# Scores of two heads per step, a shorter way out of the router, and the last norm's vector by DMA, in a one-core transformer kernel

## The chip, the cores and the metric

The kernel runs on one core of one Trainium2 chip. The metric is the device time of one execution in microseconds. Engines are named as in the profile: PE (TensorE matmuls), PEld (its weight loads), DVE (VectorE), ACT (ScalarE), POOL (GpSimd) and SP (SyncE, which issues nearly all the DMAs). In the rows below a matmul of 32-bit operands leaves two records, so a count of x32 stands for 16 matmuls.

## The reference, cut to what matters

256 tokens of width 1024 pass a first block (a forget-gate attention of 16 heads, two squared-ReLU feed-forwards, a latent attention) and a second one (a gated unit with a differential attention of 4 heads, an attention into 256 memory tokens, and 32 experts). All is float32.

```python
# first block, the mixer that the change touches (16 heads of 64)
proj = h @ w_in;  cum = jnp.cumsum(jax.nn.log_sigmoid(f_logit), axis=1)
s = jnp.einsum('bqhd,bkhd->bhqk', q_blk, k) * scale
s = s + jnp.transpose(c_blk, (0, 2, 1))[..., None] - c_keys[:, :, None, :]   # then causal softmax, @ v
...
# second block, differential attention: two softmax maps per head, 64 wide
s = jnp.einsum('bhiqd,bhikd->bhiqk', qb, k)
a = p[:, :, 0] - lam * p[:, :, 1]
...
# experts: top-1 of 4 groups, top-2 of the 8 experts in it
pg = jax.nn.softmax(t @ w_rg + b_rg);  gate_g, gidx = lax.top_k(pg, 1)
el = (t @ w_re + b_re).reshape(N, N_GROUPS, EXPERTS_PER_GROUP)[jnp.arange(N), gidx[:, 0]]
pe_top, eloc = lax.top_k(jax.nn.softmax(el), TOP_K)
wts = gate_g * pe_top / jnp.sum(pe_top)
out = sum_k wts[k] * ((silu(x @ w_gate[e]) * (x @ w_up[e])) @ w_down[e])
...
return rms_norm_2(x + out, norm_final)      # the last norm, with its gain vector of 1024
```

## The kernel before, in words

**Dense part (0 to about 834 us).** Activations lie feature-major, 8 chunks of 128 features by 256 tokens. Weights stream in 2 MB chunks through slots of SBUF; SP issues the loads (L395) as slots come free. Each 128x1024 weight block is split into a high half (ACT, `wh`, L420) and a low half (DVE or POOL, `wl`, L426), and PE forms three products per block (L455 to L457).

**Forget-gate attention (`fox`, L777).** Loop over 8 pairs of heads. For a pair PE projects the keys (`fk`, both heads stacked on 128 partitions), a pipeline step runs, PE projects the queries (`fq`), and another step runs. A step takes from each head in flight one stage of four: scores and exponentials (`sa`), normalisation (`sn`), transposes (`sb`), values (`sc`, once per pair). Before, each step holds the scores of one head: `qk_rows` (L623) issues one matmul of 128x128 (L628) and one of 128x256 (L630) on the 64 partitions of that head, into one PSUM bank of the four called `acc`. DVE adds the head's bias `fb` (made ahead on POOL in one of 4 buffers, L797 to L800) and takes the maximum (L595), ACT exponentiates (L597). The differential attention (L1181) issues the scores of its two 64-wide halves in the same way, one half behind the other, in one step.

**Router's end and the first experts (`moe`, L1449).** Behind the logits PE runs ten matmuls that nothing reads (`warm`, L400, line L404), while DVE finds the group and the two experts of each token: `place` (L1467) compares all pairs of n values (is-equal, is-greater), masks the ties, adds the two and sums. The result `asg` goes to PE for the ranks inside the experts (L1500 to L1502); DVE makes the 0/1 matrix `oh` that picks tokens into 32 rows per expert for four experts at once (L1540); PE sums the norms (`slot_rstd`) and gathers the tokens (L1533, 16 matmuls into two banks), DVE scales the gathered rows into `xg` (L1535), then makes the gate weights `wt` and `ow` (L1564 to L1555). `weigh(0)` has PE carry these to the rows (L1513) before the first expert.

**Experts.** Each of 32 experts has three loads of 2 MB (gate, up, down), 96 in all. Eleven slots exist; each is refilled when PE has read it. For an expert: `inner` twice (gate and up, L1620, 16 matmuls), `summed` (L1633), `hidden` (L1636), `permute` (L1609), `down` in two halves (L1653), with results split into `yh` (ACT) and `yl` (DVE); the results are added in four accumulating banks by `combine` (L1667), one expert later. The last expert's loads are cut into 12 parts of 512 KB. After expert 29 `gains` (L1684) spreads the last norm's gain vector over 128 partitions with 8 matmuls against scaled identities; in the last expert there are two warm matmuls before each half of `down`. `finish` (L1698) squares, multiplies by the gain, finds the inverse root, scales and stores two tiles of 512 KB.

The order on each engine is the order in which the code issues it; semaphores are inserted where tiles are shared.

Of the kernel before, what the change touches and what calls it, by code (L numbers as in the profile page):

```python
# [19 lines left out]
D = 1024  # L20
# [16 lines left out]
WARM = dict(router=10, rank=2, hidden=2, down=2)  # L37
# [131 lines left out]
PA.add("gf", 8)  # L169
# [18 lines left out]
def params(i):  # L188
# [23 lines left out]
    put(pa, PA, "gf", feature_major(i["norm_final_2"]))  # L212
# [46 lines left out]
def pack(i):  # L259
# [17 lines left out]
    return dict(wd=wd, we=we, xt=turned(i["x"]), memt=turned(i["mem_2"]), pa=pa, pb=pb, ca=ca, cb=cb, cd=cd)  # L277
# [28 lines left out]
class Program:  # L306
# [279 lines left out]
    def scores(self, qk, bias, st=None):  # L586

        nc = self.nc
        s = self.bank("acc", [128, 384])
        qk(s)  # L590
        l = self.t("L", [128, 384], bufs=2)
# [39 lines left out]

    def run(self):
# [22 lines left out]
        for name in ("sq", "sqt", "ln", "rb", "rmem", "z", "st", "xh", "xl", "memk", "b0"):  # L655
            self.home[name] = self.base
        dense = self.open("dense")
# [119 lines left out]
    def fox(self):  # L777
# [14 lines left out]

        def head(h, q, k, bc, state):
            o = 64 * (h % 2)

# [5 lines left out]

            def sa():
                state[h] = self.scores(lambda s: self.qk_rows(s, [(q[o:o + 64], k[o:o + 64])]), b)
# [304 lines left out]
    def second(self):  # L1108
# [72 lines left out]
        def head(h, q, k):  # L1181
            state = {}

            def sa():
                st = state["s"] = self.t("st2", [128, 12], bufs=3)
                for i in range(2):
                    state[i], _ = self.scores(
                        lambda s: self.qk_rows(s, [(q[64 * i:64 * i + 64], k[64 * i:64 * i + 64])]), ali[:, h],
                        (st[:, 0:4], st[:, 4:8])[i])
# [259 lines left out]
    def moe(self):  # L1449
# [77 lines left out]
        def gather(xg, ohs, rs, n):  # L1527

            for b in range(2):
                p = self.bank("pp", [128, 4, n])  # L1530
                for m in range(4 * b, 4 * b + 4):
                    for t in range(2):
                        mm(p[:, m % 4], xs[:, t, m * 128:m * 128 + 128], ohs[t], start=t == 0, stop=t == 1)  # L1533
                for m in range(4 * b, 4 * b + 4):
                    v.scalar_tensor_tensor(xg[:, m], p[:, m % 4], self.pcol("ffn2", m), rs, op0=OP.mult, op1=OP.mult)  # L1535

        def onehot(e0):
# [9 lines left out]
            gather(xg, [f[:, t] for t in range(2)], rw[:, 0], 128)  # L1547
# [54 lines left out]
        weigh(0)  # L1602

# [42 lines left out]
        def down(w, h, warm=0):  # L1646

            yh, yl = self.t("yh", [128, 1024], F32R), self.t("yl", [128, 1024], F32R)
            for half in range(2):
# [7 lines left out]
                if warm and not half:  # L1657
                    self.warm(warm)
# [23 lines left out]
        r = self.t("fr", [128, 2, 5])  # L1682

        def gains(tag, pool):  # L1684

            g = self.t("gf", [128, 8, 128], tag=tag, pool=pool)
            for half in range(2):
                p = self.bank("ps", [128, 512])
                for j in range(4):
                    d = self.t("gd", [128, 128], tag="sqt", bufs=2)  # L1690
                    v.tensor_scalar(d, self.cst("ident"), self.pcol("gf", 4 * half + j), None, op0=OP.mult)
                    mm(p[:, j * 128:j * 128 + 128], ones, d, start=True, stop=True)
                nc.scalar.copy(g[:, 4 * half:4 * half + 4].rearrange("p a b -> p (a b)"), p)
            return g.rearrange("p a b -> p (a b)")
# [3 lines left out]
        def finish():  # L1698


            def total(t, half):
                c = halves[half]
                sq = self.t("sqo", [128, 512], tag="gs0")
                nc.scalar.activation(sq, comb[t][half], AF.Square, accum_out=r[:, t, half:half + 1])
                v.tensor_mul(o[:, t, c], comb[t][half], gf[:, c])

            def norm(t):
                self.inverse(r[:, t, 3:4], r[:, t, 2:3], D, EPS, r[:, t, 4:5])

            def both(t):  # L1710
                v.tensor_add(r[:, t, 2:3], r[:, t, 0:1], r[:, t, 1:2])

            def scale(t):
                for half, c in enumerate(halves):
                    if t > half:
                        nc.scalar.mul(o[:, t, c], o[:, t, c], r[:, t, 3:4])
                    else:
                        v.tensor_scalar(o[:, t, c], o[:, t, c], r[:, t, 3:4], None, op0=OP.mult)
                nc.sync.dma_start(self.out[t * 128:t * 128 + 128], o[:, t])

            total(0, 0)
            total(0, 1)
            both(0)
            ln = self.inverse_begin(r[:, 0, 3:4], r[:, 0, 2:3], D, EPS, r[:, 0, 4:5])
            total(1, 0)
            total(1, 1)
            ln()
            both(1)
            scale(0)
            norm(1)  # L1730
            scale(1)

# [3 lines left out]
        for e in range(NE):  # L1736
# [107 lines left out]
```

## Time and profile before

| | us |
|---|---|
| median of 3 runs (lowest to highest) | 1298.98 (1298.26 to 1300.97) |
| the profiled execution | 1301.46 |
| its span, first to last instruction | 1299.8 |
| PE busy | 1218.3 (94%) |
| DVE busy | 655.7 (50%) |
| ACT busy | 525.1 (40%) |
| POOL busy | 185.3 (14%) |
| share of the span on the chain that ended last: PE, DVE, DMA | 75%, 9%, 8% |

The page's row of DMA throughput (40 slices of 32.5 us) shows 426 GB/s in most slices from 880 us on, and between 113 and 344 GB/s before. The busy shares are means over stages with different limits: in the dense part PE is nearly always busy, in the experts' part the DMA engines are. How long a wait lasts is read in the stage itself. Weight loads (PEld) overlap the matmuls.

### The profile page before, as it was taken

Reading aid. Unit: us, or ns where it says so; the run is one execution under the profiler, and the core shown is the slowest. Engines: PE = TensorE matmul, PEld = TensorE weight load, DVE = VectorE, ACT = ScalarE, POOL = GpSimd, SP = SyncE. Lnnn points to the kernel's source line nnn. Section 1 sums busy time; section 2 is a strip of 40 time slices with the busy share of each in tenths; the row PEclk is TensorE's granted clock in tenths of the full one; section 3 lists DMA queues with packets and bytes.
Section 4 is the critical chain, followed back from the end, with each engine's and each line's share of the span. In section 5 each row is a group of like instructions: output and inputs, shape, how many; then the busy total and the mean of one; then the engine's idle time right before and its main releaser. Section 6 shows DMA issues by size and latency. Waiting matters only on the chain.

```text
span 1299.8 us, 22284 instructions
## 1 busy us (share of the span) xinstructions
PE 1218.3 (94%) x9292; PEld 986.8 (76%) x9292; DVE 655.7 (50%) x1243; ACT 525.1 (40%) x982; POOL 185.3 (14%) x183
## 2 busy tenths in 40 slices
PE   7999999999989999999989999978999999897986
PEld 7788899999988899999978898944545545544443
DVE  6756666545677575655678875332222222122213
ACT  4645564544554564554555554211121121121213
POOL 4167210000152010000274210100000000000000
PEclk9999999999999999999999999999999999897978
DMA  9453445445433335544455348869999999999994
GB/s 340 192 217 113 165 155 195 157 174 205 178 132 121 126 134 195 195 156 177 187 190 190 136 165 344 333 274 426 426 426 425 424 427 424 426 424 426 427 419 160
DMA packets 30230, 338.10 MB, mean 260 GB/s; under 512 B 3488, under 2 KB 3760, under 8 KB 8112
## 3 DMA queue, kind: packets, MB, share of 16 engines
q1 hardware_dynamic: 30128, 336.66, 65.1%
q8 instruction: 74, 1.21, 0.4%
q14 instruction: 28, 0.23, 0.0%
HBM read 335.58 MB, written 1.06 MB: 259 GB/s over the span
## 4 chain that ended last, share of the span: by engine, by line
PE 75%; DVE 9%; DMA 8%; POOL 3%; ACT 2%; issue 2%; SPq 0%; DVEq 0%; POOLq 0%; ACTq 0%
PE pp L456 9%; PE pp L455 9%; PE pp L457 9%; DMA ring<-in_we_dram 8%; PE pp L1620 7%; PE acc L457 4%; PE acc L456 4%; PE acc L455 4%; PE ps L1633 4%; PE acc L1667 3%; PE pp L1533 3%; PE ps L1653 2%; DVE wl L426 2%; POOL x L900 1%; PE acc L630 1%
## 5 line engine op out<-in xcount | busy, mean ns | idle before, releaser
L426 DVE TENSOR_TENSOR wl<-ring,wh 128x1024 fp32r<-128x1024 f32 (+1 forms) x244 | 304.4, 1252 | 70.7 <-ACT wh L420 70.7
L420 ACT CAST wh<-ring 128x1024 fp32r<-128x1024 f32 (+1 forms) x246 | 252.5, 1029 | 137.5 <-PE acc L456 92.1
L457 PE MATMUL pp<-xh,wl 128*128 128x256 f32 x800 | 226.3, 283 | 1.7 <-DVE wl L426 1.7
L455 PE MATMUL pp<-xh,wh 128*128 128x256 f32 x800 | 227.3, 284 | 0.1
L456 PE MATMUL pp<-xl,wh 128*128 128x256 f32 x800 | 226.5, 283 | 0.3 <-DVE xl L515 0.3
L455 PE MATMUL acc<-hh,wh 128*128 128x256 f32 x560 | 160.0, 286 | 6.7 <-ACT hh L514 6.7
L456 PE MATMUL acc<-hl,wh 128*128 128x256 f32 x560 | 160.9, 287 | 0.7 <-DVE hl L515 0.7
L457 PE MATMUL acc<-hh,wl 128*128 128x256 f32 x560 | 159.8, 285 | 0.6 <-DVE wl L426 0.6
L455 PEld LDWEIGHTS pp<-xh,wh 128*128 128x128 f32 x800 | 151.9, 190 | 2.1 <-issue 1.7
L457 PEld LDWEIGHTS pp<-xh,wl 128*128 128x128 f32 x800 | 150.3, 188 | 1.9 <-DVE wl L426 1.9
L456 PEld LDWEIGHTS pp<-xl,wh 128*128 128x128 f32 x800 | 150.3, 188 | 0.7 <-DVE xl L515 0.6
L1620 PE MATMUL pp<-ring,xg 128*32 128x512 f32 x1024 | 123.4, 620 | 14.1 <-DMA ring<-in_we_dram 11.1
L455 PEld LDWEIGHTS acc<-hh,wh 128*128 128x128 f32 x560 | 108.8, 194 | 6.7 <-ACT hh L514 6.7
L456 PEld LDWEIGHTS acc<-hl,wh 128*128 128x128 f32 x560 | 108.4, 194 | 1.8 <-DVE hl L515 1.7
L457 PEld LDWEIGHTS acc<-hh,wl 128*128 128x128 f32 x560 | 108.8, 194 | 0.8 <-DVE wl L426 0.8
L1624 DVE COPY gs<-pp 128x512 f32<-128x512 f32 x32 | 22.1, 692 | 166.3 <-PE pp L1620 166.3
L1620 PEld LDWEIGHTS pp<-ring,xg 128*32 128x32 f32 x1024 | 30.9, 112 | 88.1 <-issue 81.5
L1633 PEld LDWEIGHTS ps<-ca,gs 128*128 128x128 f32 x512 | 64.8, 205 | 25.8 <-issue 25.4
L1656 DVE TENSOR_TENSOR yl<-ps,yh 128x512 fp32r<-128x512 f32 x64 | 44.3, 692 | 72.8 <-ACT yh L1655 72.8
L456 PE MATMUL pp<-hl,wh 128*128 128x256 f32 x272 | 77.6, 285 | 2.7 <-DVE hl L515 2.2
L455 PE MATMUL pp<-hh,wh 128*128 128x256 f32 x272 | 79.1, 291 | 0.8 <-DVE x L900 0.8
L457 PE MATMUL pp<-hh,wl 128*128 128x256 f32 x272 | 77.2, 284 | 0.7 <-DVE wl L426 0.7
(380 smaller groups left out, 1975.6 us busy)
## 6 DMA issues: line engine op xcount, KB each, us to landing
ring<-in_we_dram SPq DMA_DIRECT2D x76, 2048.0 KB, 29.1
ring<-in_wd_dram SPq DMA_DIRECT2D x58, 2048.0 KB, 8.2
ring<-in_we_dram SPq DMA_DIRECT2D x34, 1024.0 KB, 28.8
ring<-in_we_dram SPq DMA_DIRECT2D x12, 512.0 KB, 14.4
bc<-cdr SPq DMA_DIRECT2D x8, 256.0 KB, 6.3
ring<-in_wd_dram SPq DMA_DIRECT2D x1, 1792.0 KB, 6.8
ring<-in_wd_dram SPq DMA_DIRECT2D x1, 1536.0 KB, 10.8
pb<-in_pb_dram SPq DMA_DIRECT2D x1, 1152.0 KB, 10.7
```

The source lines that it names most:

```text
L420: self.nc.scalar.copy(h[:, :n], w)
L426: eng.tensor_sub(l[:, :n], w, h[:, :n].bitcast(F32))
L455: mm(out, wh, xh, start=start, stop=False, skip_group_check=skip)
L456: mm(out, wh, xl, start=False, stop=False, skip_group_check=skip)
L457: mm(out, wl, xh, start=False, stop=stop, skip_group_check=skip)
L1533: mm(p[:, m % 4], xs[:, t, m * 128:m * 128 + 128], ohs[t], start=t == 0, stop=t == 1)
L1620: mm(p[32 * j:32 * j + 32], xg(k), w(k * 512, k * 512 + 512), start=k < 4, stop=k > 3, tile_position=(0, 32 * j))
L1624: v.tensor_copy(g, p)
L1633: mm(p[:, f], g[:, f * 128:f * 128 + 128], self.cst("fold"), start=True, stop=True)
L1653: mm(p[32 * j:32 * j + 32], h[:, j], w(o, o + 512), start=True, stop=True, tile_position=(0, 32 * j))
L1656: v.tensor_sub(yl[:, c], p, yh[:, c].bitcast(F32))
L1667: mm(acc[t][half], pe[:, t * 128:t * 128 + 128], y[:, half * 512:half * 512 + 512], start=start and not i, stop=stop and i == 1, skip_grou ...
```

## The change

Five edits, all in the order and grouping of work; what is computed stays.

- Scores: a new `qk_pair` issues, for both heads of a pair, the two 128x128 products and then the two 128x256 products, each head on its own 64 partitions and into its own `acc` bank. In `fox` the even head's step does it for both heads and runs both softmaxes; the odd head's step holds no scores. The differential attention uses it for its two halves.
- Router's end: five warm matmuls instead of ten; `place` puts both comparisons in one tile and sums it, without the add; the first gather uses four banks (two of `pp`, two of `ps`) instead of two; `weigh(0)` moves behind the first expert's `inner`.
- Beginning: six warm matmuls before the first projection.
- Last expert: `combine` runs through both token tiles for `yh`, then for `yl`; the warm matmuls before the two halves of `down` are gone, and three stand before each of the two `inner`.
- Last norm: `gains` and its copies are gone; the vector is loaded by one DMA that repeats a row of 4 KB on 128 partitions, issued on SP behind the last weights. `finish` is reordered, and the second tile is stored in two halves, one issued by ACT.

```diff
-WARM = dict(router=10, rank=2, hidden=2, down=2)
+WARM = dict(start=6, router=5, rank=2, last=3)
...
+    def qk_pair(self, q, k):
+        mm = self.nc.tensor.matmul
+        s = [self.bank("acc", [128, 384]) for _ in range(2)]
+        for a, b, n in ((0, 128, 128), (128, 384, 256)):
+            for i in range(2):
+                r = slice(64 * i, 64 * i + 64)
+                mm(s[i][:, a:b], q[r, a:a + 128], k[r, 0:n], start=True, stop=True)
+        return s
...
             def sa():
-                state[h] = self.scores(lambda s: self.qk_rows(s, [(q[o:o + 64], k[o:o + 64])]), b)
+                if h % 2 == 0:
+                    for i, s in enumerate(self.qk_pair(q, k)):
+                        state[h + i] = self.softmax(s, bias[h + i])
...
         def place(name, vals, n):
-            eq, gt = (self.t(name + i, [128, 2, n, n], tag=f"gs{j}") for j, i in enumerate("eg"))
+            both = self.t(name + "e", [128, 2, n, 2 * n], tag="gs0")
+            eq, gt = both[:, :, :, :n], both[:, :, :, n:]
...
-            v.tensor_add(gt, gt, eq)
-            v.tensor_reduce(cnt, gt, axis=AX.X, op=OP.add)
+            v.tensor_reduce(cnt, both, axis=AX.X, op=OP.add)
...
-            gather(xg, [f[:, t] for t in range(2)], rw[:, 0], 128)
+            gather(xg, [f[:, t] for t in range(2)], rw[:, 0], 128, *([("pp", "pp", "ps", "ps")] if e0 == 0 else []))
...
-        weigh(0)
...
             for half in range(2):
-                for t in range(2):
-                    for i, y in enumerate(ys):
+                for i, y in enumerate(ys):
+                    for t in range(2):
                         mm(acc[t][half], pe[:, t * 128:t * 128 + 128], y[:, half * 512:half * 512 + 512], ...
...
+            square(0, 0)
+            square(1, 0)
+            square(0, 1)
+            gain(0, 0)
+            first(0)
+            gain(1, 0)
+            first(1)
+            gain(0, 1)
+            estimate(0)
+            square(1, 1)
+            mean(0)
+            gain(1, 1)
+            newton(0)
+            scale(0, 0, v)
+            scale(0, 1, v)
+            store(0, slice(0, 1024), nc.sync)
+            estimate(1)
+            mean(1)
+            newton(1)
+            scale(1, 1, nc.scalar)
+            scale(1, 0, v)
+            store(1, halves[1], nc.scalar)
+            store(1, halves[0], nc.sync)
...
             for i in range(2):
+                if last:
+                    self.warm(WARM["last"])
                 gs.append(inner(i, w[i], lambda k: xg[:, k, c]))
                 self.load_next(slots[i][1])
...
+            if e == 0:
+                weigh(0)
             h = hidden(gs, rw[:, 1, c])
...
-                self.warm(WARM["hidden"])
...
-                gf = gains(*next(p for _, s in slots for p in s if p[1] is not self.base))
+                gf = self.t("gf", [128, 1024], tag="cd")
+                nc.sync.dma_start(gf, bass.AP(tensor=self.a["gr"].tensor, offset=self.a["gr"].offset,
+                                              ap=[[0, 128], [1, D]]))
```

In `finish`, `square` is ACT's squared sum, `gain` DVE's product with the vector, `first`, `mean` and `newton` are DVE steps on one column, and `estimate` is ACT's logarithm and exponential.

PE in the fox stage, before: the scores of the first two heads (`fk`, `fq`), one head per step, between the projections (`xh`, `xl` with `wh`, `wl`).

```order
L457 MATMUL pp<-xh,wl 128x256
L628 MATMUL acc<-fk,fq 128x128
L630 MATMUL acc<-fk,fq 128x256
L455 MATMUL pp<-xh,wh 128x256
...
L457 MATMUL pp<-xh,wl 128x256
L628 MATMUL acc<-fk,fq 128x128
L630 MATMUL acc<-fk,fq 128x256
L455 MATMUL pp<-xh,wh 128x256
```

The same place now: the scores of a pair in one step (lines are shifted by the edit, L641 is `qk_pair`, L612 the transposes of an earlier head).

```order
L456 MATMUL pp<-xh,wl 128x256
L641 MATMUL acc<-fk,fq 128x128 x2
L641 MATMUL acc<-fk,fq 128x256 x2
L454 MATMUL pp<-xh,wh 128x256
...
L456 MATMUL pp<-xh,wl 128x256
L641 MATMUL acc<-fk,fq 128x128 x2
L641 MATMUL acc<-fk,fq 128x256 x2
L612 MATMUL acc<-ca,P 128x128 x3
```

The second group of the second piece belongs to the next pair: between the two, 16 blocks of projections run where 8 ran before.

PE at the router's end, before: warm matmuls, ranks, norms of the picked rows, gather, weights of the rows (`ow`), first expert.

```order
L404 MATMUL pp<-ones 128x256 x10
L1500 MATMUL ps<-asg,ca 128x32
L1501 MATMUL ps<-asg,ones 128x32
L1502 MATMUL ps<-asg,ca 128x32
L404 MATMUL pp<-ones 128x256 x2
L1513 MATMUL ps<-oh,rc 128x128 x2
L1533 MATMUL pp<-oh,xs 128x128 x16
L1513 MATMUL ps<-ow,ones 128x128 x2
L1620 MATMUL pp<-ring,xg 32x512 x16
```

And now.

```order
L403 MATMUL pp<-ones 128x256 x5
L1515 MATMUL ps<-asg,ca 128x32
L1516 MATMUL ps<-asg,ones 128x32
L1517 MATMUL ps<-asg,ca 128x32
L403 MATMUL pp<-ones 128x256 x2
L1528 MATMUL ps<-oh,rc 128x128 x2
L1549 MATMUL pp<-oh,xs 128x128 x8
L1549 MATMUL ps<-oh,xs 128x128 x8
L1634 MATMUL pp<-ring,xg 32x512 x16
L1528 MATMUL ps<-ow,ones 128x128 x2
```

The two matmuls that wait for `ow` have changed places with the first expert's 16.

PE in the last expert, before (without the combines).

```order
L1620 MATMUL pp<-ring,xg 32x512 x16
L1633 MATMUL ps<-ca,gs_12128 128x32 x4
L1633 MATMUL ps<-ca,gs_12139 128x32 x4
L1609 MATMUL pp<-ca,oh 32x128 x8
L404 MATMUL pp<-ones 128x256 x2
L1653 MATMUL ps<-ring,sh 32x512 x4
L404 MATMUL pp<-ones 128x256 x2
L1653 MATMUL ps<-ring,sh 32x512 x4
```

And now.

```order
L403 MATMUL pp<-ones 128x256 x3
L1634 MATMUL pp<-ring,xg 32x512 x8
L403 MATMUL pp<-ones 128x256 x3
L1634 MATMUL pp<-ring,xg 32x512 x8
L1647 MATMUL ps<-ca,gs_12105 128x32 x4
L1647 MATMUL ps<-ca,gs_12120 128x32 x4
L1623 MATMUL pp<-ca,oh 32x128 x8
L1667 MATMUL ps<-ring,sh 32x512 x8
```

The four warm matmuls ahead of the halves of `down` have become six ahead of the halves of `inner`; the row `L1692 MATMUL ps<-gd,ones 128x128 x8` of `gains`, two experts earlier, is gone.

## Rows read from the trace of the kernel before

**Rows 1.** Windows: stretch and length, busy of PE, PEld, DVE, ACT, POOL, PEclk, DMA, GB/s.
```profile
76.00:170.00 94.00, 94.00 (x682) 81.15 (x681) 57.98 (x163) 49.80 (x119) 49.59 (x48) 1.00 0.40 152
...
850.50:854.00 3.50, 3.50 (x20) 1.08 (x23) 0.00 (x0) 0.27 (x1) 0.00 (x0) 0.52 0.00 0
...
858.00:1126.00 268.00, 245.14 (x2033) 133.87 (x2036) 71.83 (x165) 52.88 (x114) 0.00 (x0) 0.97 1.01 425
...
1246.00:1264.00 18.00, 16.29 (x82) 10.28 (x75) 4.77 (x13) 2.99 (x6) 0.00 (x0) 0.53 1.00 419
...
1278.00:1280.10 2.10, 2.10 (x23) 1.26 (x15) 0.69 (x1) 0.07 (x1) 0.00 (x0) 1.00 0.29 115
1280.10:1290.00 9.90, 7.81 (x56) 4.07 (x55) 3.42 (x7) 5.26 (x12) 0.00 (x0) 1.00 0.01 3
```

**Rows 2.** Timeline (start us, us, engine, line, operation, count), PE, first head of the fox stage.
```profile
83.92 0.28 PE L456 MATMUL pp<-xl,wh 128*128 128x256 f32 x1
84.04 0.28 PE L457 MATMUL pp<-xh,wl 128*128 128x256 f32 x1
84.26 0.48 PE L628 MATMUL acc<-fk,fq 64*128 64x128 f32 x2
84.58 0.59 PE L630 MATMUL acc<-fk,fq 64*128 64x256 f32 x2
85.11 0.39 PE L455 MATMUL pp<-xh,wh 128*128 128x256 f32 x1
```

**Rows 3.** Timeline, PE, both halves of one head of the differential attention.
```profile
696.25 0.50 PE L628 MATMUL acc<-fk,fq 64*128 64x128 f32 x4
696.58 0.61 PE L630 MATMUL acc<-fk,fq 64*128 64x256 f32 x4
697.12 0.38 PE L455 MATMUL pp<-xh,wh 128*128 128x256 f32 x1
```

**Rows 4.** Timeline, DVE at the beginning of the program.
```profile
8.71 5.06 DVE L515 SCALAR_TENSOR_TENSOR hl<-memx,pa,hh 128x256 fp32r<-128x256 f32 x6 [0.51 <-ACT hh L514]
```

**Rows 5.** Timeline, router's end and first slot release, all engines.
```profile
834.00 5.96 PE L404 MATMUL pp<-ones 128*128 128x256 f32 x20
...
837.54 0.23 DVE L1492 TENSOR_TENSOR asg<-og,o 128x64 f32<-128x64 f32 x1
...
849.75 0.43 DVE L1555 TENSOR_TENSOR ow<-oh,wt 128x256 f32<-128x256 f32 x1
...
854.50 25.39 SPq L395 DMA_DIRECT2D ring<-in_we_dram  x8
```

**Rows 6.** Chain that ended last, in order of time (start us, us, what), from the router on.
```profile
842.16 3.59 PE pp L1533 x32
851.10 5.04 PE pp L1620 x32
860.82 3.43 PE pp L1620 x32
...
1257.45 4.73 PE ps L1692 x16
1264.77 3.57 PE pp L1620 x32
1275.42 3.57 PE pp L1620 x32
```

**Rows 7.** The same chain in the last 25 us.
```profile
1281.46 1.06 PE pp L404 x4
...
1283.52 1.06 PE pp L404 x4
1284.58 1.04 PE ps L1653 x8
...
1293.53 0.72 ACT o L1716
```

**Rows 8.** Timeline, SP, both stores of the output.
```profile
1293.07 1.55 SPq L1719 DMA_DIRECT2D out_dram<-o  x2
```

More of the change, by code (lines that the diff above doesn't have):

```diff
@@ L168 @@
 PA.add("rbias", 36)
-PA.add("gf", 8)
 PB = Columns()
@@ L586, in scores, with softmax @@
     def scores(self, qk, bias, st=None):
-        nc = self.nc
         s = self.bank("acc", [128, 384])
         qk(s)
+        return self.softmax(s, bias, st)
+    def softmax(self, s, bias, st=None):
+        nc = self.nc
         l = self.t("L", [128, 384], bufs=2)
@@ L656, in run @@
             self.home[name] = self.base
+        self.warm(WARM["start"])
         dense = self.open("dense")
@@ L1185, in sa @@
                 st = state["s"] = self.t("st2", [128, 12], bufs=3)
[L1186 to L1189, printed above, removed]
+                for i, s in enumerate(self.qk_pair(q, k)):
+                    state[i], _ = self.softmax(s, ali[:, h], st[:, 4 * i:4 * i + 4])
             def sn():
@@ L1525, in slot_weight, with gather @@
             nc.scalar.copy(dst, p)
[L1527 to L1531, printed above, removed]
+        def gather(xg, ohs, rs, n, banks=("pp", "pp")):
+            w = 8 // len(banks)
+            for b, bank in enumerate(banks):
+                p = self.bank(bank, [128, w, n])
+                for m in range(w * b, w * b + w):
                     for t in range(2):
-                        mm(p[:, m % 4], xs[:, t, m * 128:m * 128 + 128], ohs[t], start=t == 0, stop=t == 1)
-                for m in range(4 * b, 4 * b + 4):
-                    v.scalar_tensor_tensor(xg[:, m], p[:, m % 4], self.pcol("ffn2", m), rs, op0=OP.mult, op1=OP.mult)
+                        mm(p[:, m % w], xs[:, t, m * 128:m * 128 + 128], ohs[t], start=t == 0, stop=t == 1)
+                for m in range(w * b, w * b + w):
+                    v.scalar_tensor_tensor(xg[:, m], p[:, m % w], self.pcol("ffn2", m), rs, op0=OP.mult, op1=OP.mult)
         def onehot(e0):
@@ L1644, in hidden, with down @@
             return sh[:, 1]
-        def down(w, h, warm=0):
+        def down(w, h):
             yh, yl = self.t("yh", [128, 1024], F32R), self.t("yl", [128, 1024], F32R)
@@ L1656, in down @@
                 v.tensor_sub(yl[:, c], p, yh[:, c].bitcast(F32))
-                if warm and not half:
-                    self.warm(warm)
             return yh, yl
@@ L1681, in moe @@
         o = self.t("o", [128, 2, 1024], tag="b0")
[L1682 to L1694, printed above, removed]
+        r = self.t("fr", [128, 2, 6])
@@ L1696, in moe, with square @@
         halves = slice(0, 512), slice(512, 1024)
         def finish():
-            def total(t, half):
-                c = halves[half]
+            def square(t, half):
                 sq = self.t("sqo", [128, 512], tag="gs0")
                 nc.scalar.activation(sq, comb[t][half], AF.Square, accum_out=r[:, t, half:half + 1])
-                v.tensor_mul(o[:, t, c], comb[t][half], gf[:, c])
-            def norm(t):
-                self.inverse(r[:, t, 3:4], r[:, t, 2:3], D, EPS, r[:, t, 4:5])
@@ L1710, in both @@
[L1710 to L1731, printed above, removed]
+            def gain(t, half):
+                v.tensor_mul(o[:, t, halves[half]], comb[t][half], gf[:, halves[half]])
+            def first(t):
+                v.tensor_scalar(r[:, t, 2:3], r[:, t, 0:1], 1.0 / D, EPS, op0=OP.mult, op1=OP.add)
@@ new lines, in estimate, with newton @@
+            def estimate(t):
+                nc.scalar.activation(r[:, t, 4:5], r[:, t, 1:2], AF.Ln, bias=r[:, t, 2:3], scale=1.0 / D)
+                nc.scalar.activation(r[:, t, 3:4], r[:, t, 4:5], AF.Exp, scale=-0.5)
+            def newton(t):
+                e, tmp = r[:, t, 3:4], r[:, t, 4:5]
+                v.scalar_tensor_tensor(tmp, r[:, t, 5:6], 0.0, e, op0=OP.add, op1=OP.mult)
+                v.scalar_tensor_tensor(tmp, tmp, -0.5, e, op0=OP.mult, op1=OP.mult)
+                v.scalar_tensor_tensor(e, tmp, 1.5, e, op0=OP.add, op1=OP.mult)
@@ new lines, in mean, with scale, store @@
+            def mean(t):
+                v.scalar_tensor_tensor(r[:, t, 5:6], r[:, t, 1:2], 1.0 / D, r[:, t, 2:3], op0=OP.mult, op1=OP.add)
+            def scale(t, half, eng):
+                z = o[:, t, halves[half]]
+                if eng is v:
+                    v.tensor_scalar(z, z, r[:, t, 3:4], None, op0=OP.mult)
+                else:
+                    nc.scalar.mul(z, z, r[:, t, 3:4])
+            def store(t, c, eng):
+                eng.dma_start(self.out[t * 128:t * 128 + 128, c], o[:, t, c])
@@ L1757, in moe @@
                 weigh(e + 3)
-            prev = (pe, down(w[2], h, WARM["down"] if last else 0))
+            prev = (pe, down(w[2], h))
             self.load_next(slots[2][1])
```

9 lines of the change are left out of this document (5 added, 4 removed).

## The prediction, made before the changed kernel ran

> **What bounds the kernel now.** I read the windows first, stage by stage, then the timeline at the places that the change touches, then the chain of waits from the router on. From 76 to 170 us, the stage of the 16 heads, PE is busy for 94.00 of 94.00 us at full clock, DVE for 57.98, POOL for 49.59 [rows 1]: every microsecond of PE that goes there moves all that follows. From 858 to 1126 us the DMA share is 1.01 at 425 GB/s while PE is busy for 245 of 268 us [rows 1]: here the stream of expert weights sets the pace. So the experts' end is the time at which that stream restarts, plus its length. It restarts late: in 850.5 to 854 nothing is moved [rows 1], because all eleven slots are full until PE has read the first one, and SP issues the next load at 854.50 [rows 5]. Behind the last weights (1280.1, where 115 GB/s fall to 3 [rows 1]) stands PE's last expert and the last norm, to the span's end at 1299.8.
>
> **The change part by part.** All against the profiled execution, 1301.46 us.
>
> *Scores in the 16-head stage.* Projections follow one another by 0.12 us (83.92 to 84.04). Around one head's scores the distance is 85.11 − 84.04 = 1.07, so a group costs 0.95; its own four records take 85.11 − 84.26 = 0.85 [rows 2]. The changed step holds eight records on both row halves. The trace has just that: the differential attention's step, whose two halves stand one behind the other, takes 697.12 − 696.25 = 0.87 for eight records [rows 3], 0.02 more than four. So a pair costs 0.97 where two heads cost 1.90, and eight pairs give 8 × 0.93 = 7.4 us. Bounds: 8.6 if an odd step's whole 1.07 went; 0.8 if the two heads ran one after the other (0.85 more per pair). I take 7.4, the row of eight records. For the differential attention itself that row says 0: its halves already run together. DVE and POOL must keep up: the same work as before in 94 − 7.4 = 86.6 us, 67% and 57% busy on average, but DVE gets two heads at once. The scores' banks are the same four.
>
> The Trainium skill, "TensorEngine Tiling (Array Packing)", PSUM Bottleneck, warns that packing speeds up TensorE alone and the PSUM copy may then be what is late. By it the 7.4 would shrink towards the lower bound, and the total would be 1284.6 at worst. DVE's 57.98 of 94 us [rows 1] leaves room on average; no row here shows DVE with two heads of this stage at once.
>
> *Beginning.* Six warm matmuls run before PE's first projection. The first projections are paced by DVE, which makes the low halves of the memory tokens until 8.71 + 5.06 = 13.77 [rows 4]. A faster PE waits for that: 0. Bounds: −0.5 to +1.5 (a clock that falls again in those waits).
>
> *Router's end.* PE issues in order: 20 records of warm until 834.00 + 5.96 = 839.96, while `asg` is ready at 837.54 + 0.23 = 837.77 [rows 5]; the ranks wait for the warm. With ten records the warm ends between 834.00 + 2.98 (half the time) and later, since the early ones are the slow ones; I estimate 837.3. `place` loses an add twice and sums twice as many elements; by `asg`'s 0.23 per instruction that is 0.2 to 0.46, so `asg` comes at about 837.4. The ranks move from 839.96 to 837.5: −2.5 (bounds −2.6 to −1.5).
>
> Behind the gather (842.16 + 3.59 = 845.75) the first expert does not begin before 851.10 [rows 6]: PE's queue holds the two matmuls that need `ow`, ready at 849.75 + 0.43 = 850.18 [rows 5]. Now the 16 matmuls of `inner` stand ahead of them and need the gathered rows alone, which come in four banks, the last a pair of scalings behind the gather. They begin some 0.2 behind it: 5.1 us less (bounds 4.2 if the last rows are late, to 5.3). Together `inner` begins 7.6 us earlier. It ran at 0.52 of the clock [rows 1], after PE had stood waiting, 5.04 us against 3.43 for a later one [rows 6]. Without that stop I take the full clock. The first slot is free after half of `inner`: 3.4 behind its begin before (854.50 − 851.10), 1.7 now (half of 3.43). SP's queue sees the release 7.6 + 1.7 = 9.3 earlier. Bounds: −9.6, and −5.7 if the clock is slow there as well (1.5 + 4.2).
>
> `ow` now comes about 4.4 us (850.18 − 845.75) behind the gather and `inner` ends 3.6 behind it, so PE stands up to 0.8 us before the weights of the rows. Behind it in the queue are `summed`, `down` and with it the third slot release, for which the stream has two loads of 2.1 MB, 4.9 us each at 425 GB/s, as cover. Later releases come with PE, 7.6 earlier and not 9.3: cover shrinks by up to 1.7 us. I put +0.5 (0 to 1.5) for a gap in the stream.
>
> *The stream.* 96 − 11 = 85 loads × 4.93 = 419 us at a DMA share of 1.01: nothing in the change shortens it. It begins 7.4 + 9.3 − 0.5 earlier, and so the last weights land at about 1280.1 − 16.2 = 1263.9.
>
> *Last expert.* I keep the old time axis, with the weights at 1280.1. `gains` held PE for 4.73 us [rows 6] and some 1 us of waiting before it. Two times two warm matmuls cost 2 × 1.06 [rows 7]. Twelve records of warm are new: 3 × 1.06 = 3.2 at full clock. PE's own chain ends 4.73 + 1 + 2.12 − 3.2 = 4.6 earlier than 1284.58 + 1.04 = 1285.62, at 1281.0. The data set another floor: the last 2.1 MB are `down`, so `up` is there at 1280.1 − 4.9 = 1275.2; from there half an `inner` (1.8), the stretch from `inner`'s end 1278.99 to `down` without its warm (1282.52 − 1278.99 − 1.06 = 2.5) and two halves (2.1) give 1281.6. The later of the two is the data's; I take 1281.7, −3.9. Bounds −4.6 and +1: in 1246 to 1264 the clock was 0.53 [rows 1], and if it stays there through both last experts the twelve records cost 6.4 and `inner` 1.6 more each.
>
> *Last norm.* The vector's transfer is queued behind the last weights: 0.5 MB at 425 GB/s lands 1.2 us behind them, 1281.3, before DVE's first product, which now stands behind the first square at about 1283.5. It hides; without that cover up to 1 us. From `down`'s end to the first store's issue were 1293.07 − 1285.62 = 7.5 us [rows 7, 8], to the end of the last scaling 1294.25 − 1285.62 = 8.6. By the lengths of the same instructions the new order gives 7.0 and 8.4, and the last transfers are half as long (half of 512 KB at 425 GB/s is 0.6). I take −1.1 (−2.5 to +0.5).
>
> Sum: −7.4 − 9.3 + 0.5 − 3.9 − 1.1 = −21.2, so 1280.3. The profiled execution was 2.5 above the median; against the median that is 1278.
>
> **The rivals.**
>
> *Scores give nothing.* DVE gets two heads' maxima and sums at once, falls behind, and PE waits for a free `acc` bank in each pair, or the banks conflict. For: two heads land together. Against: rows 3, with both halves' softmaxes in one step. At the lower bound 0.8 instead of 7.4: 1284.6.
>
> *The stream is not carried along.* The slots after the first three come free by PE's pace in experts 0 to 4, not by the first release; then the stream starts 9.3 earlier and stops again. At 7.6 less 2 for the late `ow` and its followers, the gain is 5.6 instead of 8.8: 1281. Against: 425 GB/s from 858 on.
>
> *The end stays slow.* With `gains` gone PE does less in experts 29 and 30, the clock stays at its lower level and the last expert ends as before or 1 later: 1278 + 4 to 5 = 1282.5.
>
> *Slower: the experts run at the lower clock for long.* The matmuls of `inner` take 5.04/3.43 = 1.47 times as long there [rows 6]. Between 858 and 1126 PE has 245 us of work in 268 [rows 1], 23 to spare; a share x of the stretch at the lower clock adds 0.47 × 245 × x = 115x. Up to a fifth of it is free, from 38% on (44 us, 21 of them not covered) the whole gain is gone, and at a half 57 − 23 = 34 are lost: 1312. PE then releases the slots too late and the stream stops behind it. For: half of the warm work ahead of the experts is gone, so is `gains`, and 1246 to 1264 shows 0.53 [rows 1]. Against: 0.97 on average in 858 to 1126, with pauses that the change does not touch.
>
> The Trainium skill, "TensorE: Matmul & The Clock Gate", HAM oscillation, says that a PE that waits for data again and again pays the return to the full clock each time; that is the rule behind this rival. The 0.52 behind the wait before 851 agrees with it, and the 0.97 of the first twenty experts speaks against it there.
>
> **How the numbers follow.** Forecast (its own range 1273 to 1284, from −25 to −14): 0.66. Scores give nothing 0.08, stream not carried along 0.07, end slow 0.09, slower 0.07, and 0.03 that several of them together leave no difference. What a measurement of this kernel tells from no change is about 0.2%, 2.6 us; the first four cases lie far beyond it. Range 1271 to 1289. Faster 0.90, same 0.03, slower 0.07.
>
> **What would show it.** Scores: eight groups of eight records in some 0.87 each, PE still busy throughout, and everything at 170 us 7.4 earlier; PE idle before L641 or a wait on DVE would refute it. Router: ranks right behind `asg`, `inner` right behind the gather at full clock, SP's first issue 16.7 earlier than 854.50 (near 837.8). Stream: 425 GB/s from there without a gap, last weights near 1264. End: `down` done 1.6 behind the weights, no wait for the vector, last store issued 8.4 later. A stop of the DMA engines after the first loads, or a clock below 0.9 over the first twenty experts, would make the forecast wrong.

## The result and the profile after

The changed kernel takes 1283.53 us (median of 4 runs, 1280.73 to 1283.62), the kernel before beside it 1299.97 (1298.26 to 1302.23): ratio 0.9867, 95% interval 0.9846 to 0.9889. It is 16 us faster; 1278 was forecast, in a range of 1271 to 1289. The profiled execution took 1283.50, its span is 1281.8 against 1299.8. The difference of the two spans, stage by stage (a minus is a gain):

| stage, and how it is measured in both traces | before | after | change | forecast |
|---|---|---|---|---|
| beginning: start of the 240th projection product (counted from 0, here and below) | 81.29 | 81.31 | +0.0 | 0 |
| 16 heads: from there to the 640th | 87.35 | 79.38 | −8.0 | −7.4 |
| opening of the latent attention: 2320th to 2480th | 28.82 | 30.92 | +2.1 | 0 |
| other dense stages, to the 5120th | | | +0.1 | 0 |
| router's end: from there to SP's first load | 35.05 | 26.08 | −9.0 | −9.3 |
| stream: first load to last load's issue | 415.5 | 416.9 | +1.4 | +0.5 |
| last expert: last load's issue to the end of `down` | 15.6 | 11.5 | −4.1 | −3.9 |
| last norm: to the end of the span | 14.2 | 13.7 | −0.5 | −1.1 |
| sum | | | −18.0 | −21.2 |

The counted products are the 5196 records of the dense projections, equally many in both traces. PE's timeline in the stage of the 16 heads, after (it answers to [rows 2]); L641 is `qk_pair`:

```profile
84.07 0.28 PE L456 MATMUL pp<-xh,wl 128*128 128x256 f32 x1
84.28 0.93 PE L641 MATMUL acc<-fk,fq 64*128 64x128 f32 x8
85.14 0.39 PE L454 MATMUL pp<-xh,wh 128*128 128x256 f32 x1
```

Eight records stand where four stood: 85.14 − 84.07 = 1.07, exactly the distance of one head before. So a pair costs nothing more than a head, and an odd step's group is gone. PE is busy throughout the stage (columns as in [rows 1]):

```profile
76.00:163.00 87.00, 87.00 (x690) 77.96 (x689) 61.89 (x164) 50.70 (x120) 44.03 (x48) 1.00 0.45 164
```

Where the stage and the next attention end is read from the values' matmuls, first before, then after (count, ns min/median/max, first and last start):

```profile
L619 PE MATMUL acc<-PT,fv x32: 379/379/431, 101.8 to 163.2; 128*64 128x256 f32 x32
L619 PE MATMUL acc<-PT,v x16: 378/380/382, 442.4 to 452.1; 128*128 128x256 f32 x16
```

```profile
L621 PE MATMUL acc<-PT,fv x32: 379/379/431, 99.8 to 155.3; 128*64 128x256 f32 x32
...
L621 PE MATMUL acc<-PT,v x16: 379/380/382, 436.5 to 446.3; 128*128 128x256 f32 x16
```

The 16 heads end 7.9 earlier (163.2 to 155.3), the latent attention, 290 us further on, only 5.8 (452.1 to 446.3). No edit touches the stretch between. The router's end, after (answers to [rows 5] and the first rows of [rows 6]), all engines:

```profile
828.23 3.72 PE L403 MATMUL pp<-ones 128*128 128x256 f32 x10
...
831.37 0.23 DVE L1507 TENSOR_TENSOR asg<-og,o 128x64 f32<-128x64 f32 x1
...
831.78 0.33 PE L1515 MATMUL ps<-asg,ca 128*128 128x32 f32 x2
...
835.80 1.95 PE L1549 MATMUL ps<-oh,xs 128*128 128x128 f32 x16
...
837.68 3.64 PE L1634 MATMUL pp<-ring,xg 128*32 128x512 f32 x32
...
842.00 0.41 DVE L1571 TENSOR_TENSOR ow<-oh,wt 128x256 f32<-128x256 f32 x1
...
842.47 0.71 PE L1528 MATMUL ps<-ow,ones 128*128 128x128 f32 x4 [1.15 <-DVE ow L1571]
```

The ranks now wait for `asg` (831.60) and no longer for the warm; `inner` follows the gather within 0.1 us and takes 3.64 where it took 5.04. PE then stands 1.15 us for `ow`. SP, after:

```profile
839.75 29.69 SPq L394 DMA_DIRECT2D ring<-in_we_dram  x10
```

The first load goes out at 839.75 instead of 854.50: 14.75 earlier, 5.8 of it from the dense part and 9.0 from here. The stretch of the stream behind it, after (columns as in [rows 1]):

```profile
846.00:856.00 10.00, 10.00 (x76) 4.75 (x69) 2.08 (x3) 2.41 (x5) 0.00 (x0) 0.89 1.00 421
856.00:866.00 10.00, 7.82 (x81) 5.77 (x84) 4.06 (x13) 1.81 (x5) 0.00 (x0) 1.00 1.00 419
866.00:876.00 10.00, 9.32 (x88) 4.81 (x76) 2.75 (x6) 2.50 (x6) 0.00 (x0) 1.00 0.97 388
```

388 instead of 425 GB/s in 866 to 876 is a stop of about 0.9 us: the seventh load is issued at 865.68, when the loads before it are nearly through (the sixth lands at 868.37). The last expert, PE, after (answers to [rows 7]):

```profile
1256.88 1.46 PE L403 MATMUL pp<-ones 128*128 128x256 f32 x6
...
1258.26 1.92 PE L1634 MATMUL pp<-ring,xg 128*32 128x512 f32 x16
...
1260.12 1.56 PE L403 MATMUL pp<-ones 128*128 128x256 f32 x6
...
1261.61 1.92 PE L1634 MATMUL pp<-ring,xg 128*32 128x512 f32 x16
...
1266.22 1.92 PE L1667 MATMUL ps<-ring,sh 128*32 128x512 f32 x16 [0.21 <-DVE sh L1657]
```

The last load is issued at 1256.68 and takes 10.1 us to land, as before (1270.00, 10.1): 1266.8. `down` ends at 1268.1, 1.3 behind it, where it ended 5.5 behind it.

### The profile page after: what moved, and what is told of

The parts are those of the page before. It is cut to its first block, busy times and chain, and to the rows that moved or that the text cites. A ratio compares the mean times of both kernels' runs of the same rounds, so it can differ in the third digit from the quotient of the medians.

```text
span 1281.8 us, 22259 instructions
## 1 busy us (share of the span) xinstructions
PE 1202.0 (94%) x9282; PEld 970.6 (76%) x9282; DVE 655.8 (51%) x1235; ACT 524.1 (41%) x980; POOL 179.9 (14%) x183
## 5 line engine op out<-in xcount | busy, mean ns | idle before, releaser
L425 DVE TENSOR_TENSOR wl<-ring,wh 128x1024 fp32r<-128x1024 f32 (+1 forms) x244 | 307.8, 1266 | 71.5 <-ACT wh L419 71.5
L1647 PEld LDWEIGHTS ps<-ca,gs 128*128 128x128 f32 x512 | 60.0, 192 | 24.3 <-issue 24.0
```

What stands on the lines that cost most here:

```text
L425: eng.tensor_sub(l[:, :n], w, h[:, :n].bitcast(F32))
L1647: mm(p[:, f], g[:, f * 128:f * 128 + 128], self.cst("fold"), start=True, stop=True)
```

## The experiments

All are edits of the changed kernel; e9 leaves it as it is, and e10 and e11 combine several edits. Ratios are to the kernel before on the same chip; where a median is set beside the changed kernel's 1283.53, the two were measured apart. The times of a kernel spread by 2 to 8 us from run to run, so terms are read from the stages of the profiles, and the medians stand beside them.

**e1_no_pairs**:

```diff
-                if h % 2 == 0:
-                    for i, s in enumerate(self.qk_pair(q, k)):
-                        state[h + i] = self.softmax(s, bias[h + i])
+                o = 64 * (h % 2)
+                state[h] = self.scores(lambda s: self.qk_rows(s, [(q[o:o + 64], k[o:o + 64])]), b)
```

> The changed kernel, with one head's scores per step again. Theory A (scores are a saving of PE time that nothing else hides): each group of four records costs 1.07 us from projection to projection again, the end of the 16-head stage comes 7.9 us later than in the changed kernel, and so do the ranks, the first slot release and the last weights, less what the opening of the latent attention gives back by chance: +6 to +8 us, 1289 to 1292. Theory B (the 2.1 us that the changed kernel lost at the opening of the latent attention, near 380 us, are caused by the paired scores): the loss is gone here, so the router begins only 5.8 later than in the changed kernel, as in the kernel before. Theory A's form of it: the loss there is set by where the low clock and a long DVE instruction fall, and can be anything between 0 and 3 us in this run.

Median 1292.23 (1290.13 to 1297.95, 10 runs), ratio 0.9934 (0.9917 to 0.9952). Its stage of 16 heads takes 87.35 us, as before: the pairs are worth 8.0 there. Its beginning was 1.7 later than the changed kernel's, and the opening of the latent attention took 28.86: none of the 2.1 was lost. That speaks for theory B as well as for A's chance, and is taken up by the next runs, which all keep the pairs.

**e2_weigh_first**:

```diff
-            if e == 0:
-                weigh(0)
...
+        weigh(0)
+
         def permute(ohs):
```

> The changed kernel, with the first expert's row weights ahead of its first 16 matmuls again. Theory A (PE stood behind the two matmuls that wait for the weights, and lost its clock there): the first expert begins 4.3 to 5.1 us later, at the lower clock, SP's first load behind the stop comes 6 to 7 us later, and the end moves by as much less the 1 us that the stream loses now near 866: +5 to +7, 1288 to 1291. Theory B (the release of the first slot doesn't set the end, because later slots come free by PE's own pace): the end moves by 2 us or less.

Median 1288.31 (1285.15 to 1288.86), ratio 0.9908 (0.9883 to 0.9933): 4.8 above the changed kernel. PE, from the second half of the gather on (the first half begins at 831.40):

```profile
833.18 1.95 PE L1549 MATMUL ps<-oh,xs 128*128 128x128 f32 x16
839.11 1.22 PE L1528 MATMUL ps<-ow,ones 128*128 128x128 f32 x4 [3.97 <-DVE ow L1571]
840.26 4.59 PE L1636 MATMUL pp<-ring,xg 128*32 128x512 f32 x32
```

From the gather's begin to `inner` are 8.9 us against 3.7 in the changed kernel, 5.2 more; `inner` runs slow again (4.59), and from the gather's begin to SP's first load are 11.8 against 5.7, 6.1 more. The stream gave 1.2 back (415.7 from first to last load, 416.9 in the changed kernel). Theory A, and two thirds of the router's 9.0. Here, with the same dense code as in the changed kernel, the opening of the latent attention took 28.89: the pairs alone don't force the loss. Windows of that opening, in the changed kernel and then in this run, each from some 13 us behind the 2320th product:

```profile
376.00:380.00 4.00, 1.84 (x13) 1.42 (x12) 4.00 (x4) 1.06 (x3) 2.44 (x1) 1.00 0.00 0
380.00:384.00 4.00, 3.37 (x16) 3.37 (x17) 2.02 (x6) 1.76 (x3) 0.00 (x0) 0.57 0.67 193
```

```profile
375.50:379.50 4.00, 1.67 (x14) 1.47 (x14) 4.00 (x4) 1.05 (x3) 3.21 (x1) 1.00 0.00 0
379.50:383.50 4.00, 4.00 (x34) 4.00 (x35) 1.88 (x6) 2.73 (x6) 0.00 (x0) 1.00 0.91 287
```

In both PE stands for more than half of the first 4 us and waits for DVE's low halves. In the changed kernel's profile the clock then falls to 0.57, and 16 records pass where 34 do in the other; e2's lower clock lies earlier in the opening, and the changed kernel's has that one too. Over the whole opening the granted clock is 0.94 in e2 and 0.89 in the changed kernel. The other difference is the place of one of DVE's low halves that takes 2.6 us; POOL and DVE, changed kernel:

```profile
376.32 2.44 POOL L425 TENSOR_TENSOR wl<-ring,wh 128x1024 fp32r<-128x1024 f32 x1 [2.85 <-ACT wh L419]
```

```profile
376.46 2.58 DVE L514 SCALAR_TENSOR_TENSOR hl<-x,pa,hh 128x256 fp32r<-128x256 f32 x1
378.97 1.21 DVE L425 TENSOR_TENSOR wl<-ring,wh 128x1024 fp32r<-128x1024 f32 x1
```

Its seven like take 0.47. It begins 0.14 behind a split on POOL and ends 0.28 behind that one's end. In this profile DVE's next `wl` stands behind it; in e2's the `wl` stands ahead of it, as in all the other profiles. How the 2.1 divides between the clock and this order was not tried.

**e3_router_ten**, a single run: `router=5` back to `router=10`.

> The changed kernel, with ten warm matmuls at the router's end again. Theory A (they only delay the ranks, PE's queue being in order): ranks, gather, first expert and first load all 2.2 to 2.5 us later, end +2.3. Theory B (they keep the clock up for what follows): the first four experts spend less time at the lower clock, and the end moves by 0 or is earlier.

1285.16, span 1283.4. From the 5120th projection to the gather are 22.6 us against 20.3: the five matmuls delay the ranks by 2.2, as in theory A. The stream takes 415.5 from first to last load instead of 416.9, so the end gets less than the 2.2. What theory B says of the clock was seen as well: over the first 35 us behind the first load it is 1.00 here and 0.95 in the changed kernel, whose first expert has its `down` at the lower level, and the stop of the stream is gone. First expert's `down`, changed kernel and then this run, and this run's stream:

```profile
845.78 3.05 PE L1667 MATMUL ps<-ring,sh 128*32 128x512 f32 x16
```

```profile
848.67 1.92 PE L1667 MATMUL ps<-ring,sh 128*32 128x512 f32 x16 [0.27 <-DVE sh L1657]
866.00:876.00 10.00, 9.79 (x96) 5.23 (x92) 2.66 (x5) 2.41 (x5) 0.00 (x0) 1.00 1.00 416
```

That the five more matmuls keep the clock there is not shown by one profile.

**e4_down_first**:

```diff
-            if e % 4 == 1 and e + 3 < NE:
+            if e % 4 == 1 and e + 3 < NE and e > 1:
                 onehot(e + 3)
                 weigh(e + 3)
             prev = (pe, down(w[2], h))
             self.load_next(slots[2][1])
+            if e == 1:
+                onehot(e + 3)
+                weigh(e + 3)
```

> The changed kernel, with the preparation of experts 4 to 7 moved behind the down product of expert 1 (it stands ahead of it in both kernels). Theory A (the stream stops for about 1 us near 866 because the sixth slot is released only when that preparation is done): the sixth load is issued near 857 instead of 865.7, the stream runs at 425 GB/s throughout, the last weights land 1 us earlier, the end is 0.8 to 1.2 earlier, 1282.4. Theory B (the dip is the DMA engines' own): no change.

Median 1284.53 (1283.63 to 1285.46): no gain. The seventh load is issued at 856.0, as theory A had it, but the next stands 11.9 behind it, and the stop only moves and grows:

```profile
856.00:866.00 10.00, 6.54 (x44) 6.28 (x47) 4.10 (x12) 0.85 (x2) 0.00 (x0) 0.83 1.03 433
866.00:876.00 10.00, 9.79 (x89) 5.05 (x88) 1.40 (x4) 2.09 (x5) 0.00 (x0) 1.00 0.95 365
876.00:886.00 10.00, 6.57 (x44) 2.71 (x41) 3.85 (x14) 1.17 (x2) 0.00 (x0) 0.83 0.97 397
```

365 and 397 GB/s are 2.1 us lost, in an execution whose first load went out at 836.97. Theory A named the wrong term: not one slot, but PE's pace through the first experts, as e8 then shows. The order and the clock are not told apart here: it was at 0.83 in 836 to 846 and again in 856 to 866.

**e5_start_none**: `start=6` to `start=0`.

> The changed kernel, without the six warm matmuls before the first projection. Five profiles of kernels with them put the 240th projection at 80.6 to 83.3 us, the kernel before at 81.3. Theory A (they raise the clock too early; PE then waits for DVE, the clock falls again, and where it falls decides between 80.6 and 83.3): without them the 240th projection stands near 81.3, and the median is within 1.5 us of the changed kernel, either way. Theory B (they are worth something, as placed): without them 1 us or more slower. Theory C (they hurt on average): 1 us or more faster.

Median 1282.91 (1281.85 to 1284.15), ratio 0.9859 (0.984 to 0.9878); the 240th projection at 80.75. The median is the same within the spread: theory A. In the profiles the six matmuls rather cost: the 240th projection stands at 80.6 to 83.3, on average 82.2, in the nine profiles that have them and no filling (e10), and at 80.8 in e11, without them.

**e6_last_none**: `last=3` to `last=0`.

> The changed kernel, without the two times three warm matmuls in the last expert. Theory A (they hold the clock until the weights are there, and cost PE 1.5 us each, of which the wait for the weights hides most): the down product cannot end before the last part lands, about 1266.8 on the changed kernel's axis, so at most 1.3 us are to be had; expected between 1 us faster and 2 slower, the latter if PE falls to the lower clock at the end. Theory B (the last expert is bound by PE's own chain): the full 3 us faster.

Median 1283.02 (1280.16 to 1284.09), ratio 0.985 (0.9829 to 0.987). From the last load's issue to the end of `down` are 11.15 us against 11.46: 0.3 and not 3, theory A. Eight more profiles with the changed kernel's last expert give 11.2 to 12.8, so the 0.3 itself is not clear of the spread. The six matmuls fill time in which PE waits for weights.

**e7_gains_on_pe**, a single run: the transfer replaced by `gains` of the kernel before, the rest as changed.

> The changed kernel, with the last norm's vector made by 8 matmuls after expert 29 again in place of the transfer. Theory A (these hold PE for 4.7 us and its waits, and PE's chain then ends later than the weights): PE's last expert begins 4 to 5 us later relative to the last load, the end is 3 to 4 us later. Theory B (PE has that time to spare, since experts 30 and 31 wait for weights): 1 us or less.

1288.3, span 1286.5. PE:

```profile
1243.83 4.71 PE L1706 MATMUL ps<-gd,ones 128*128 128x128 f32 x16 [1.72 <-DVE gd L1705]
```

From the last load's issue to the end of `down` are 16.2 us against 11.5, 4.8 more: theory A. The whole gain of the last expert, 4.1, is that of these eight matmuls; the moved warm matmuls give nothing beside it.

**e8_onehot_at_three**: as e4, with the preparation behind the `down` of expert 3.

> The changed kernel, with the preparation of experts 4 to 7 behind the down product of expert 3 instead of ahead of that of expert 1. In the run that moved it behind the down product of expert 1 the stop of the stream did not vanish but moved to the next release. Theory A (PE's pace in experts 0 to 3 is what the slots wait for; the work must go where several loads are queued): no stop between the first load and the last, first load to last issue 415.5 us or less against 416.9, the end about 1.5 earlier relative to the first load. Theory B (PE is later with experts 0 to 3 whatever the order): a stop of 1 us or more stays.

Median 1282.97 (1281.31 to 1283.66), ratio 0.9852 (0.9834 to 0.9871). The stop is gone:

```profile
866.00:876.00 10.00, 6.35 (x55) 2.61 (x58) 3.86 (x15) 1.69 (x4) 0.00 (x0) 0.86 1.01 429
```

From the first to the last load are 416.0 us instead of 416.9: theory A, a little short of its number. The same code without this edit took 416.9 to 418.8 (changed kernel, e1, e5, e6, e7, e9). The beginning of this execution was 1.8 later than the changed kernel's, which hides the gain in the span.

**e9_changed_again**: no edit.

> The changed kernel once more, unaltered. Theory A (the beginning and the opening of the latent attention end at one of a few times, set by where the lower clock and one long DVE instruction fall in the execution): the stretch from the 2320th to the 2480th projection is 28.8, 29.6 or 30.9 us in this profile, the 240th projection anywhere between 80.6 and 83.4, and the time within 2 us of 1283.5. Theory B (both are a fixed property of the kernel): 30.9 and 81.3 again.

Median 1284.12 (1281.10 to 1286.67), ratio 0.9872 (0.9852 to 0.9892). The 240th projection stands at 82.98 and the opening took 29.57, against 81.31 and 30.92: theory A. Over all profiles of these kernels the opening took 28.8 to 28.9 (five), 29.5 to 29.6 (seven) or 30.9 (one, the changed kernel's first); the granted clock of the opening is 0.94 in the first five and 0.88 to 0.89 in the others. Of the five, two hold no pairs (the kernel before, e1) and three do; the other eight all do. So the execution decides, and whether the pairs make the longer openings more frequent is open.

**e10_filled**: e8 with PE's waits filled.

```diff
+            if fill and i < nk - 1:
+                self.nc.tensor.matmul(fill, self.ones[:, :128], self.ones[:, :128], start=True, stop=True)
...
-            p = self.proj("mk", mn, banks="pp" if m in (4, 5) else "acc")
+            p = self.proj("mk", mn, banks="pp" if m in (4, 5) else "acc", fill=self.bank("pp", [128, 128]) if m == 0 else None)
...
+        self.warm(5)
         for c in range(3):
             p = self.proj("kva", src, order=TURNS)
```

> The changed kernel with PE's waits filled: a matmul of 128 columns that nothing reads between the products of the first block, where PE waits for DVE, and five warm matmuls where PE waits for DVE at the opening of the latent attention; and the preparation of experts 4 to 7 behind expert 3. Theory A (the clock falls there because PE waits, and a filled wait keeps it): full clock from 8 us on, the 240th projection at 80.6, the stretch of the latent attention 28.8 to 29.6, no stop of the stream; together 1.5 to 3 us faster than the changed kernel, 1280.5 to 1282. Theory B (the extra matmuls delay PE more than the clock gives back): the 240th projection at 82 or later and no gain.

Median 1280.45 (1279.23 to 1281.43), ratio 0.9843 (0.9828 to 0.9859), span 1279.7: 3.7 below the changed kernel measured beside it (e9), more than expected, and all five of its runs lie below the changed kernel's median there. The beginning in e1 (its PE code up to there is the changed kernel's) and then in this run:

```profile
12.00:16.00 4.00, 3.67 (x15) 3.05 (x14) 4.00 (x5) 2.00 (x2) 3.84 (x5) 0.50 0.90 378
16.00:20.00 4.00, 4.00 (x23) 4.00 (x23) 3.74 (x3) 1.09 (x2) 3.92 (x3) 0.57 0.95 314
```

```profile
12.00:16.00 4.00, 3.04 (x22) 2.53 (x21) 4.00 (x4) 1.99 (x2) 3.84 (x5) 1.00 1.00 394
16.00:20.00 4.00, 4.00 (x36) 4.00 (x35) 4.00 (x4) 2.00 (x2) 3.92 (x3) 1.00 0.92 360
```

With the waits filled the clock stays at its upper level and 36 records pass where 23 did; the 240th projection stands at 80.72. e1 is one of the late starts, but all nine profiles with the six matmuls and no filling show a lower clock here, and e11 gets the same from no warm matmuls at all (80.80). In the opening of the latent attention the clock was 1.00 in 376 to 384, but 0.63 in 364 to 368 and 0.52 in 368 to 372, ahead of the five matmuls at 375.47: they stood behind the fall that they were to prevent. The opening took 29.58, as in the runs without them: nothing is gained there.

**e11_plain_start**: e8 with `start=0` and `last=1`.

> The changed kernel without the warm matmuls at the beginning, with one instead of three ahead of each half of the last expert, and with the preparation of experts 4 to 7 behind expert 3. Theory A: beginning as in the kernel before within 0.6 us, no stop of the stream (1 us), last expert 0.3 to 1 us shorter against the weights: 1 to 2 us faster than the changed kernel, about 1282. Theory B (the last expert needs its warm matmuls to hold the clock): its end 2 us or more later against the last load, no gain.

Median 1281.00 (1279.73 to 1282.47), ratio 0.9855 (0.9836 to 0.9873). The stream takes 415.5, as in theory A; `down` ends 11.3 behind the last load's issue, 0.2 less than in the changed kernel, where 0.3 to 1 was expected. By their medians both runs lie below the changed kernel, e10 lowest; the interval of e11 overlaps that of e9 by half, that of e10 only at its edge, and e10 and e11 are not told apart.

## Why the prediction came out as it did

- *Scores.* Right in mechanism, 8.0 for 7.4. A pair takes 1.07 from projection to projection, not 1.09, and the odd steps lose their group whole: 0.95 in the first, and 1.00 in each of the seven where transposes follow the group (from the projection before to the one behind 1.36 before, 0.36 after), a case that [rows 2] didn't show. That is 7.95, and the 0.6 above the forecast hid part of the losses below by chance. DVE (61.89 of 87 us) and POOL (44.03) kept up, and PE was busy for 87.00 of 87.00 us from 76 to 163. The warning of the Trainium skill, "TensorEngine Tiling (Array Packing)", PSUM Bottleneck, did not come true here.
- *Beginning.* 0.03 in the first profile, −0.6 to +2.1 in the others: wider than the stated bounds. The reason given, a clock that falls again in DVE's waits, is what the profiles show: over 8 to 20 us it is 0.57 to 0.86 in the nine with the six matmuls and no filling, 1.00 in e10.
- *What follows the 16 heads moves with it.* This is the step that was missing a term: 2.1 of the 8.0 were lost at the opening of the latent attention. The prediction took PE as the bound of the whole dense part from the window of one stage. Near 376 us PE waits for DVE, and what is lost there varies with the execution: 30.9 and 29.6 in two profiles of the same kernel. In 12 of 13 profiles the loss is 0.8 or less, so the first profile was the worst case.
- *Router's end.* Right in place and size: ranks −2.2 for −2.5, `inner` −7.6 for −7.6, first load −9.0 for −9.3; e2 and e3 split it into 6.1 and 2.2; the other 0.7 (`place`, the four banks) was not tried alone.
- *Stream.* The gap was sized at 0.5 and was 1.4, at the upper bound. The stop of the DMA engines that was named as a sign against the forecast came, but small. The rival that the stream is not carried along had this mechanism: e4 and e8 show that in experts 0 to 3 PE's pace, not one slot, sets when loads go out. The clock is part of that pace: the four profiles with a granted clock of 1.00 over the first 35 us behind the first load (the kernel before, e2, e3, e11) took 415.5 to 415.7 for the stream, the six with 0.95 and the changed kernel's order 416.9 to 418.8, and e4 with 0.90 took 419.7. So a first load that is brought forward alone can be paid back in part: 1.2 in e2, 1.5 in e3.
- *Last expert.* −4.1 for −3.9. The argument by the landing of the weights held (e6), and `gains` is the term that counts (e7). The rival of a slow end did not come: the clock was 1.00 in 1255 to 1262.
- *Last norm.* −0.5 for −1.1, in a stage that took 13.1 to 14.1 us in the other runs without `gains`. From `down`'s end to the first store's issue were 7.0 us, as worked out; the last store is issued 8.5 behind it, not 8.4, and the shorter last transfers bring less than the 0.6 counted. The vector's transfer, issued at 1258.02, landed some 10 us later at 1268.0, ahead of DVE's first product at 1270.44.
- *Clock in the experts.* The slower rival did not come at its size: 0.97 in 858 to 1126 as before, and the fall behind the router's stop is gone. It comes a little later instead (0.89 in 846 to 856, behind the wait for `ow`), and the small stop of the stream goes with it. The rule of the Trainium skill, "TensorE: Matmul & The Clock Gate", HAM oscillation, that waits cost the clock, was at work elsewhere, at the beginning and near 380 us, where PE waits for DVE and not for data. The trace agrees with it only in part: in the kernel before, e5 and e11 PE has such waits at the beginning too, and the clock is 1.00 from 8 to 20 us. Why it falls only behind the warm matmuls is open.

In sum −18.0 for −21.2 in the profiles: 2.1 from the opening, 0.9 from the stream, 0.6 from the last norm, 0.3 from the router, 0.1 from the other dense stages, less 0.6 from the scores and 0.2 from the last expert. The medians differ by 16.4, because the profiled execution of the kernel before (1301.46) lies 1.5 above its median and that of the changed kernel at its own.

## What to carry to other kernels

A gain in a stage where an engine is never idle goes through to the end only if no later stage waits for another engine; look for those before counting it whole. In an engine's queue it is the order that costs: two matmuls that wait for a late vector, ahead of sixteen that don't, were worth 6 us. When a stopped stream is restarted earlier, count the slots that come free after the first, by the pace, and the clock, of what reads them.

## What was not expected of the hardware

- Eight matmul records on two halves of the rows take 0.86 us from the first to the next projection, no more than four on one half (0.85).
- Warm matmuls ahead of work that waits can leave PE worse off: in e1 and e3 the clock was 0.50 to 0.57 from 12 to 20 us, and the 240th projection stood at 83.0 and 83.3, against 80.75 to 81.3 without them. The same stretch in e9 with them and in e5 without:

```profile
8.00:20.00 12.00, 10.97 (x47) 9.66 (x47) 10.97 (x11) 6.65 (x11) 11.61 (x12) 0.57 0.96 380
```

```profile
8.00:20.00 12.00, 11.30 (x67) 10.42 (x67) 10.32 (x11) 7.50 (x11) 11.59 (x12) 1.00 1.01 392
```

- In the opening of the latent attention one of eight like DVE instructions takes 2.58 us instead of 0.47, while POOL splits a weight block beside it (376.32 to 378.76). All 13 profiles have it: 2.58 to 2.65 us, begun 0.1 to 0.9 behind the begin of POOL's split and ended 0.28 to 0.29 behind its end; DVE's `wl` beside POOL's split before that takes 3.4 to 3.5 us, where the next one takes 1.2. The Trainium skill, "SBUF — State Buffer", section "SBUF: two separate sides", describes a port pair that DVE and GpSimd share as an exclusive lock, so that the later of the two waits for the whole of the other's instruction; these rows agree with it. A run with that split on another engine was not made.
